# Fifty-two weight blocks of a two-block transformer layer, multiplied as whole float32 in place of three split products

## The chip, the cores and the metric

The kernel runs on one core of a Trainium2 chip. A core has a matrix engine (PE, TensorE; its weight loads are listed as PEld), a vector engine (DVE), an activation engine (ACT), a general engine (POOL, GpSimd) and a queue that starts transfers (SP). The metric is the device time of one execution in microseconds (us); less is better.

## The reference, cut to what matters

The reference is two transformer blocks, one after the other, over 256 tokens (and 16 learned "meta" tokens) of width 1024, all in float32. The change touches only the start of the first block:

```python
u = rms_norm(h, pre_mix_gain[l])
proj = u @ w_in[l]
qa, ka, va, qb, kb, vb, g = jnp.split(proj, SPLITS, axis=-1)
...
o_swa = windowed_gqa_sink_attention(qa, ka, va, attn_sink[l], pos, is_real)
...
o_diff = differential_attention(qb, kb, vb, lam, lambda_init, diff_subln_gain[l], is_key)
gates = jax.nn.sigmoid(g + b_gate[l])
merged = g_swa * (o_swa @ w_branch_swa[l]) + g_diff * (o_diff @ w_branch_diff[l])
h = h + rms_norm(merged @ w_out[l], post_mix_gain[l])
```

`w_in` is 1024 by 6656, so 52 blocks of 1024 by 128: 8 for `qa`, 4 for `ka` and `va`, 8 each for `qb`, `kb`, `vb`, and 16 for the gates. After that come the first block's feed-forward, and the whole second block (a delta-rule mixer, a sparse attention, a cross attention, a second feed-forward), which the change leaves alone.

## The kernel before

Activations lie transposed: a tile holds 128 features by the tokens. A weight block is 128 partitions by 1024 (eight pieces of 128 by 128, one for each 128 of the contraction). `raw_w` has SP load a block into `raw` (three buffers, 512 KB a block). `load_w` then splits it into two tiles of the rounded type float32r: `wh` is the block rounded (a copy on ACT) and `wl` is the rest, `raw - wh` (on DVE, or on POOL for every second block while `wshare[0]` is 2). Activations are split in the same way by `split` into `uh` and `ul`. `gemm` multiplies each of the eight pieces three times, `wh·uh + wh·ul + wl·uh`, so 24 matmuls a block into one PSUM bank. Twenty blocks (`kb`, `vb`, `ka`, `va`) take all 272 tokens, `us_k`; 32 (`qb`, `qa`, the gates) take 256, `us`.

What stands around these blocks is attention: eight differential heads (`diff_head`) and eight pairs of window heads (`swa_pair`), in the order of `ORDER`. Each takes scores on PE (the line of `scores`), maxima on DVE, exponentials on ACT, normalised weights on DVE (`am`, `pr`), transposes on PE into PSUM tiles `t`, a split of those on ACT and DVE, and the product with the values on PE. A query or key block, once multiplied, goes through `rope` (ACT, DVE, POOL) and a split. The blocks of head n+2 are multiplied after head n, and the gate blocks fill in between, as `GATES` says. At the end of the stage `branch_d` multiplies eight blocks `w_bd` and the merge multiplies eight blocks `w_bs`, with `gemm` in both versions. A 1 MB transfer of `memt` stands on SP's queue behind the last `w_bd` block; its squares and sums on POOL (`mem_split`) end in a small matmul, in `sums_tok`.

The program is laid out for each engine before it runs: a scheduler puts the instructions of each engine in one fixed order, and semaphores make them wait for one another. The start of the stage:

```python
AHEAD = 2
for n in range(AHEAD):
    prepare(n)
for n, (t, i) in enumerate(units):
    if t == "d":
        diff_head(i, qs.pop(0))
    else:
        swa_pair(i // 4, i % 4, qs.pop(0))
    if n + AHEAD < 16:
        prepare(n + AHEAD)
    for _ in range(GATES[n]):
        gate_of(fill.pop(0))
```

Of the kernel before, what the change touches and what calls it, by code (L numbers as in the profile page):

```python
# [16 lines left out]
F32 = mybir.dt.float32  # L17
# [3 lines left out]
AF = mybir.ActivationFunctionType  # L21
# [4 lines left out]
P = 128  # L26
NT = 256
NM = 16
NK = NT + NM
NP = NT + 32  # L30
D = 1024
KT = D // P
# [173 lines left out]

WSHARE = 2
ORDER = "ddssdsddsdssddss"  # L210
GATES = [int(c) for c in "0010202020302022"]
BDLAST = 0
# [8 lines left out]
def _program(tc, d, out):  # L221
    nc = tc.nc
    ctx = ExitStack()
    pe, act, dve, pool, sp = nc.tensor, nc.scalar, nc.vector, nc.gpsimd, nc.sync
# [7 lines left out]
    with ctx:  # L232
# [4 lines left out]
        gpool = new_pool(ctx, "gen")  # L237
        mm = new_pool(ctx, "mm", 2, PSUM)


        hT = rpool.tile([P, KT, NK], F32, name="hT", tag="resA")
# [14 lines left out]
        def G(n, j=0):  # L256
            o, w = _GC[n]
            return gcol[:, o + j:o + j + 1]
# [25 lines left out]
        def split(h, l, src, gain=None):  # L284

            if gain is None:
                m = act.activation(h, src, AF.Copy)
                dve.tensor_tensor(l, src, h.bitcast(F32), OP.subtract)
            else:
                m = act.activation(h, src, AF.Copy, scale=gain)  # L290
                dve.scalar_tensor_tensor(l, src, gain, h.bitcast(F32), OP.mult, OP.subtract)  # L291
            return m

        wcount, wshare, hshare, last_w = [0], [0], [0], [None]

        def raw_w(src, n):
            raw = wpool.tile([P, KT * P], F32, name="raw", tag="raw", bufs=3)
            last_w[0] = sp.dma_start(raw[:, :n * P], src)
            return raw
# [16 lines left out]
        def gemm(src, xs, n, use, first=True, last=True, ps=None, raw=None, late=()):  # L316

            kt = len(xs)
            h, l = load_w(src, kt, raw=raw)
            if ps is None:  # L320
                ps = mm.tile([P, 512], F32, name="mm", tag="mm")
            o = ps[:, :n]
            soon = [k for k in range(kt) if k not in late]
            steps = [(w, k, i) for ks in (soon, late) for w, i2 in ((h, 2), (l, 1)) for k in ks for i in range(i2)]
            for n_, (w, k, i) in enumerate(steps):
                pe.matmul(o, w[:, k * P:(k + 1) * P], xs[k][i], start=(first and n_ == 0),  # L326
                          stop=(last and n_ == len(steps) - 1))
            if last and use is not None:
                use(o)
            return ps  # L330

        def gemm_long(src, xs, n, use):

            ps = None
            for k in range(0, len(xs), KT):
                part = xs[k:k + KT]
                ps = gemm(src[:, k * P:(k + len(part)) * P], part, n, use, first=(k == 0),
                          last=(k + KT >= len(xs)), ps=ps)
# [59 lines left out]
        def new_u():  # L398
            uh = gpool.tile([P, KT, NK], F32R, name="uh", tag="uh")
            ul = gpool.tile([P, KT, NK], F32R, name="ul", tag="ul")  # L400
            return uh, ul
# [8 lines left out]
        apx = ExitStack()  # L410
        apool = new_pool(apx, "a")

        uh, ul = new_u()

        st = opool.tile([P, 512], F32, name="st", tag="o")
        for _ in range(WARM):
            tc.keep_in_program_order(pe.matmul(st[:, :P], one.to_broadcast([P, P]), one.to_broadcast([P, P]),
                                               start=True, stop=True))
        wfirst = [raw_w(d["w_kb"][0], KT)]
        for k in range(1, KT, 2):  # L420
            n = min(2, KT - k)
# [6 lines left out]
        ipool = new_pool(ist, "i", side="right")  # L428
        st = opool.tile([P, 512], F32, name="st", tag="o")
        for k in range(KT):  # L430
            split(uh[:, k, :], ul[:, k, :], hT[:, k, :], G("pre_mix", k))
            s0 = ipool.tile([P, NK], F32, name="s0", tag="s0", bufs=KT)
            pool.tensor_tensor(s0, hT[:, k, :], hT[:, k, :], OP.mult)
            pe.matmul(st[:, :NK], ones_d, s0, start=(k == 0), stop=(k == KT - 1))
# [2 lines left out]
        dve.tensor_copy(below_b, CA("below"))  # L437
        rs = gpool.tile([P, NK], F32, name="rs", tag="rs", bufs=2)
        rsqrt_chain(st[:, :NK], NK, rs)
        us = [(uh[:, k, :NT], ul[:, k, :NT]) for k in range(KT)]  # L440
        us_k = [(uh[:, k, :], ul[:, k, :]) for k in range(KT)]
        ist.close()

        gate = apool.tile([P, 16, NT], F32, name="gate")
# [45 lines left out]
        def bank():  # L490

            began[0] += 1
            return ppool.tile([P, 512], F32, name="s", tag="s") if began[0] <= 3 else None
# [5 lines left out]
        def key(o, kh, kl, eng):  # L499
            k = kpool.tile([P, NK], F32, name="kraw", tag="kraw", bufs=3)  # L500
            rope(o, k, ckt, skt, NK, eng)
            split(kh, kl, k)
# [8 lines left out]
        def key_tiles(name, bufs):  # L511
            return [kpool.tile([P, NK], F32R, name=name + e, tag=name + e, bufs=bufs) for e in ("_h", "_l")]

        kb, vb = {}, {}

        def keys_b(h):
            kb[h] = key_tiles("kb", 3)
            gemm(d["w_kb"][h], us_k, NK, lambda o: key(o, *kb[h], dve), ps=bank(),
                 raw=wfirst.pop(0) if wfirst else None)

        def padded(name, n, shape):
# [14 lines left out]
        def value(o, h, l, m, cols=slice(0, P)):  # L536

            v = next(vTs)
            dve.tensor_tensor(v[:, :NK], o, rs, OP.mult)
            t = tpool.tile([P, 512], F32, name="t", tag="t")  # L540
            pe.transpose(t[:, 0:128], v[:, 0:128], ident)
            pe.transpose(t[:, 128:256], v[:, 128:256], ident)
            tm = tpool.tile([P, 512], F32, name="t", tag="t")
            pe.transpose(tm[:32, :P], v[:, NT:], ident)
            t3 = t[:, 0:256].rearrange("p (a b) -> p a b", a=2)
            for hh, ll_, mm_, cc_ in zip(h, l, m, cols):
                act.activation(hh, t3[:, :, cc_], AF.Copy)
                dve.tensor_tensor(ll_, t3[:, :, cc_], hh.bitcast(F32), OP.subtract)
                stacked(mm_, tm[:32, cc_], 32)

        def values_b(h):
            vh = kpool.tile([P, 2, P], F32R, name="vb_h", tag="vb_h", bufs=3)
            vl = kpool.tile([P, 2, P], F32R, name="vb_l", tag="vb_l", bufs=3)
            vm = kpool.tile([96, P], F32R, name="vbm", tag="vbm", bufs=3)
            vb[h] = vh, vl, vm
            gemm(d["w_vb"][h], us_k, NK, lambda o: value(o, [vh], [vl], [vm], [slice(0, P)]), ps=bank(),
                 raw=wfirst.pop(0) if wfirst else None)

        def probs_t(pps):
# [74 lines left out]
        def query(src):  # L634
            q = [kpool.tile([P, NT], F32R, name="q" + e, tag="q" + e, bufs=3) for e in "hl"]

            def use(o):
                qr = kpool.tile([P, NT], F32, name="qraw", tag="qraw", bufs=2)
                rope(o, qr, cqt, sqt, NT)
                split(*q, qr)  # L640
            gemm(src, us, NT, use, ps=bank())
            return q

        os_h, os_l = [None] * 8, [None] * 8
# [36 lines left out]
        ka = [key_tiles("ka%d" % p, 1) for p in range(2)]  # L681
# [6 lines left out]

        def swa_keys():
            for p in range(2):  # L690
                gemm(d["w_kva"][p], us_k, NK, lambda o, p=p: key(o, *ka[p], pool))
            lo, hi = slice(0, 64), slice(64, P)
            for p in range(2):
                gemm(d["w_kva"][2 + p], us_k, NK, lambda o, p=p: value(
                    o, [va_h[:, :, p, i, c] for i, c in ((0, lo), (1, hi))],
                    [va_l[:, :, p, i, c] for i, c in ((0, lo), (1, hi))],
                    [vam[:, p, i, c] for i, c in ((0, lo), (1, hi))], [lo, hi]))

        def gate_of(j):
            gemm(d["w_gate1"][j], us, NT,  # L700
                 lambda o: dve.tensor_tensor(gate[:, j, :], o, rs[:, :NT], OP.mult))

        ods = [(od_h[:, k, :], od_l[:, k, :]) for k in range(8)]
# [3 lines left out]
            gemm(d["w_bd"][j], ods, NT, lambda o: act.activation(bd[:, j, :], o, AF.Copy))  # L707


        wshare[0] = WSHARE  # L710
        order = ORDER
        units = [(t, order[:i].count(t)) for i, t in enumerate(order)]
        qs, fill = [], list(range(16))
# [91 lines left out]
        for j in range(8):  # L805
            def use(o, j=j):
                t = mpool.tile([P, NT], F32, name="mt", tag="mt", bufs=2)
                dve.tensor_tensor(t, o, gate[:, j, :], OP.mult)
                dve.tensor_tensor(t, t, bd[:, j, :], OP.add)
                split(m_h[:, j, :], m_l[:, j, :], t)  # L810
# [18 lines left out]
        def post_norm(src_w, xs, gain, res, res_out, g_next):  # L829
# [12 lines left out]
            for j in range(8):  # L842
# [9 lines left out]
        us, rs = post_norm(d["w_out1"], [(m_h[:, k, :], m_l[:, k, :]) for k in range(8)],  # L852
                           "post_mix", hT, h1, "pre_ffn")

        def ffn_in(pool_, src_w, us, rs, f_h, f_l):
            for j in range(FT):
# [7 lines left out]
                def use_u(o, sg=sg, j=j):  # L864
# [44 lines left out]
        us, rs = post_norm(d["w_fo1"], [(f_h[:, k, :], f_l[:, k, :]) for k in range(FT)],  # L909
                           "post_ffn", h1, x1, "g_mix")  # L910
# [549 lines left out]
        for c in range(2):  # L1460
            gb = ppool.tile([P, 512], F32, name="s", tag="s")
            for h in range(4):
                pe.matmul(gb[:, h * P:(h + 1) * P], gg[:, 4 * c + h:4 * c + h + 1].to_broadcast([P, P]), triu,
                          start=True, stop=True)
# [62 lines left out]
        us, rs = residual(d["w_out2"], [(mix_h[:, k, :], mix_l[:, k, :]) for k in range(8)], x1, x2, "g_xattn", (0,1,2,3), 2)  # L1527
# [26 lines left out]
        for h in range(4):  # L1554
# [28 lines left out]
            o = opool.tile([P, 512], F32, name="o", tag="o")  # L1583
            o = o.rearrange("p (a b) -> p a b", a=2)
# [8 lines left out]
        us, rs = residual(d["w_xo"], [(ox_h[:, k, :], ox_l[:, k, :]) for k in range(8)], x2, x3, "g_ffn", (4,5,6,7), 2)  # L1593
# [49 lines left out]
        for qb in range(2):  # L1643
# [3 lines left out]
            for n, i in enumerate(own):  # L1647
                _, lo, w = parts[i]
                cols = slice(lo, lo + w)
                x = x3t[:, qb, cols]  # L1650
# [39 lines left out]
```

## Time and profile before

| what | value |
|---|---|
| median of three runs | 1033.79 us (1032.21 to 1034.55) |
| the profiled execution | 1033.08 us, of which the span from first to last instruction is 1031.3 us |
| PE busy in the span | 964.4 us (94%) |
| DVE busy | 771.9 us (75%) |
| ACT busy | 563.9 us (55%) |
| POOL busy | 369.0 us (36%) |
| granted TensorE clock, mean | 0.976 |

Matmuls are pipelined, so their busy time is not the time that each takes in a stream; the pace of a stream is read from the starts of consecutive matmuls in a timeline. A granted clock of 1.00 is the upper of the engine's two levels, 2.4 GHz, 0.50 the lower, 1.2 GHz; a mean between them is a stretch that had some of both. The stage that the change touches runs from the start to about 264 us.

### The profile page before, as it was taken

The numbers are of one execution on the slowest core, as the hardware profiler recorded it, in microseconds if no ns is written. First come the engines' busy times: TensorE is split into PE (matmuls) and PEld (weight loads), VectorE is DVE, ScalarE is ACT, GpSimd is POOL, SyncE is SP. The second block draws the span as 40 slices with busy tenths as digits, with TensorE's granted clock in tenths as the row PEclk, the third lists the DMA queues.
The fourth block names the chain that finished last, engine by engine and source line by source line (L and its number), as shares of the span: only waits on it lengthen the run. The fifth ranks groups of instructions, "written<-read, shape, count | busy, mean of one in ns | idle before, by whom it ended". The sixth has DMA issues, their size and how long they took to land.

```text
span 1031.3 us, 19437 instructions
## 1 busy us (share of the span) xinstructions
PE 964.4 (94%) x7532; PEld 916.8 (89%) x7532; DVE 771.9 (75%) x1477; ACT 563.9 (55%) x1111; POOL 369.0 (36%) x317
## 2 busy tenths in 40 slices
PE   9889999999969999999999778769999999999997
PEld 8779899998959989999999777668899999999986
DVE  7999888888696786666456899999688686656544
ACT  5566767667445655555554555435666565555433
POOL 6866458555590221212100755553021102121002
PEclk9999999999989999999999899799999999999999
DMA  6323333332444475555665331231035255555552
GB/s 236 124 102 108 119 106 117 106 124 103 164 143 161 146 242 177 189 186 181 212 209 179 123 123 62 83 122 63 2 104 183 103 181 188 184 185 186 184 191 94
DMA packets 42027, 149.32 MB, mean 145 GB/s; under 512 B 4728, under 2 KB 5376, under 8 KB 41808
## 3 DMA queue, kind: packets, MB, share of 16 engines
q1 hardware_dynamic: 40896, 145.47, 41.2%
q0 software_dynamic: 608, 2.03, 0.7%
q8 instruction: 59, 0.97, 0.4%
q10 hardware_dynamic: 432, 0.59, 0.2%
q14 instruction: 32, 0.26, 0.1%
HBM read 147.01 MB, written 1.06 MB: 144 GB/s over the span
## 4 chain that ended last, share of the span: by engine, by line
PE 67%; DVE 22%; ACT 3%; POOL 3%; issue 3%; DMA 2%; SPq 0%; DVEq 0%; ACTq 0%; POOLq 0%
PE mm L326 46%; DVE wl L313 3%; PE s L326 2%; PE ac L1624 2%; PE s L509 2%; PE ac L1628 2%; PE ac L1627 2%; ACT wh L311 1%; DVE acc L393 1%; DVE base L1129 1%; POOL memt L773 1%; DVE fg L843 1%; DVE ul L291 1%; DVE y L981 1%; PE o L589 1%
## 5 line engine op out<-in xcount | busy, mean ns | idle before, releaser
L311 ACT ACTIVATE wh<-raw 128x1024 fp32r<-128x1024 f32 (+1 forms) x266 | 279.3, 1053 | 230.0 <-PE mm L326 138.1
L326 PE MATMUL mm<-uh,wh 128*128 128x256 f32 (+1 forms) x1272 | 322.5, 289 | 11.9 <-DVE zp L975 7.6
L313 DVE TENSOR_TENSOR wl<-raw,wh 128x1024 fp32r<-128x1024 f32 (+1 forms) x219 | 272.6, 1247 | 77.5 <-ACT wh L311 76.3
L326 PE MATMUL mm<-ul,wh 128*128 128x256 f32 (+1 forms) x1272 | 320.1, 287 | 0.0
L326 PEld LDWEIGHTS mm<-uh,wh 128*128 128x128 f32 x1272 | 242.7, 191 | 16.7 <-issue 8.3
L326 PEld LDWEIGHTS mm<-ul,wh 128*128 128x128 f32 x1272 | 243.2, 191 | 1.1 <-issue 0.2
L326 PE MATMUL mm<-uh,wl 128*128 128x256 f32 (+1 forms) x1272 | 184.5, 284 | 0.0
L326 PEld LDWEIGHTS mm<-uh,wl 128*128 128x128 f32 x1272 | 165.3, 190 | 0.9 <-issue 0.2
L313 POOL TENSOR_TENSOR wl<-raw,wh 128x1024 fp32r<-128x1024 f32 x53 | 127.7, 2415 | 90.4 <-ACT wh L311 79.6
L862 POOL TENSOR_TENSOR sg<-sg,rs 128x256 f32<-128x256 f32 x44 | 49.6, 1130 | 233.6 <-ACT sg L861 228.6
L866 DVE TENSOR_TENSOR ft<-mm,sg 128x256 f32<-128x256 f32 x42 | 17.8, 424 | 52.0 <-PE mm L326 51.4
L326 PE MATMUL mm<-f_h,wh 128*128 128x256 f32 x176 | 41.1, 276 | 0.0
L326 PE MATMUL mm<-f_l,wh 128*128 128x256 f32 x176 | 41.1, 276 | 0.0
L860 DVE TENSOR_TENSOR sg<-mm,rs 128x256 f32<-128x256 f32 x40 | 16.9, 424 | 31.8 <-PE mm L326 31.8
L1624 PE MATMUL ac<-wh,f_h 128*128 128x512 f32 (+1 forms) x110 | 38.4, 349 | 0.0
L1627 PE MATMUL ac<-wh,f_l 128*128 128x512 f32 (+1 forms) x110 | 38.1, 347 | 0.0
L1628 PE MATMUL ac<-wl,f_h 128*128 128x512 f32 (+1 forms) x110 | 37.8, 347 | 0.0
L326 PEld LDWEIGHTS mm<-f_h,wh 128*128 128x128 f32 x176 | 33.0, 188 | 0.0
L326 PEld LDWEIGHTS mm<-f_l,wh 128*128 128x128 f32 x176 | 33.0, 188 | 0.0
L844 POOL TENSOR_TENSOR x<-fg,h 128x256 f32<-128x256 f32 x8 | 8.8, 1127 | 66.6 <-DVE fg L843 66.6
L1540 POOL TENSOR_TENSOR kx_l<-kx,kx_h 128x512 fp32r<-128x512 f32 x4 | 6.8, 1720 | 66.8 <-ACT kx_h L1539 66.8
L393 DVE TENSOR_TENSOR acc<-acc,sq 128x256 f32<-128x256 f32 x42 | 27.1, 646 | 0.4
(546 smaller groups left out, 2234.9 us busy)
## 6 DMA issues: line engine op xcount, KB each, us to landing
raw<-w_gu SPq DMA_DIRECT2D x88, 512.0 KB, 3.3
raw<-w_dn SPq DMA_DIRECT2D x22, 512.0 KB, 3.2
raw<-w_pr SPq DMA_DIRECT2D x20, 512.0 KB, 3.3
raw<-w_gate SPq DMA_DIRECT2D x16, 512.0 KB, 3.2
raw<-w_out SPq DMA_DIRECT2D x16, 512.0 KB, 3.2
raw<-w_fo SPq DMA_DIRECT2D x16, 512.0 KB, 3.7
raw<-w_kb SPq DMA_DIRECT2D x8, 512.0 KB, 3.3
raw<-w_vb SPq DMA_DIRECT2D x8, 512.0 KB, 3.3
```

The lines of the kernel that those rows point to most:

```text
L291: dve.scalar_tensor_tensor(l, src, gain, h.bitcast(F32), OP.mult, OP.subtract)
L311: act.activation(h[:, :kt * c], raw[:, :kt * c], AF.Copy)
L313: eng.tensor_tensor(l[:, :kt * c], raw[:, :kt * c], h[:, :kt * c].bitcast(F32), OP.subtract)
L326: pe.matmul(o, w[:, k * P:(k + 1) * P], xs[k][i], start=(first and n_ == 0), stop=(last and n_ == len(steps) - 1))
L393: dve.tensor_tensor(acc, acc, s[:, :n], OP.add)
L509: pe.matmul(os[c], a[half[c], tok], b[half[c]], start=(n == 0), stop=(last and n == 2))
L860: dve.tensor_tensor(sg, o, rs, OP.mult)
L862: pool.tensor_tensor(sg, sg, rs, OP.mult)
L866: dve.tensor_tensor(t, o, sg, OP.mult)
L1624: m = pe.matmul(o, f_h[:, k, tok], h[:, cols], start=(k == 0), stop=False)
L1627: pe.matmul(o, f_l[:, k, tok], h[:, cols], start=False, stop=False)
L1628: pe.matmul(o, f_h[:, k, tok], l[:, cols], start=False, stop=(k == FT - 1))
```

## The change

A new function `gemm_whole` multiplies each of the eight pieces once, the raw float32 block with the whole float32 activation: eight matmuls a block in place of 24, and neither `wh` nor `wl` is made. All 52 blocks of the first block's projections go through it. The activation `u` is written by one ACT operation for each 128 features, and not split. `wshare[0]` is no longer set in this stage, so the splits of the `w_bd` blocks, which stay as they were, are all on DVE.

```diff
-WSHARE = 2
...
+        def gemm_whole(src, xs, n, use, ps=None, raw=None):
+
+            if raw is None:
+                raw = raw_w(src, len(xs))
+            if ps is None:
+                ps = mm.tile([P, 512], F32, name="mm", tag="mm")
+            o = ps[:, :n]
+            for k, x in enumerate(xs):
+                pe.matmul(o, raw[:, k * P:(k + 1) * P], x, start=(k == 0), stop=(k == len(xs) - 1))
+            use(o)
...
-        uh, ul = new_u()
+        u = gpool.tile([P, KT, NK], F32, name="u", tag="uh")
...
-            split(uh[:, k, :], ul[:, k, :], hT[:, k, :], G("pre_mix", k))
+            act.activation(u[:, k, :], hT[:, k, :], AF.Copy, scale=G("pre_mix", k))
...
-        us = [(uh[:, k, :NT], ul[:, k, :NT]) for k in range(KT)]
-        us_k = [(uh[:, k, :], ul[:, k, :]) for k in range(KT)]
+        us = [u[:, k, :NT] for k in range(KT)]
+        us_k = [u[:, k, :] for k in range(KT)]
...
-            gemm(d["w_kb"][h], us_k, NK, lambda o: key(o, *kb[h], dve), ps=bank(),
+            gemm_whole(d["w_kb"][h], us_k, NK, lambda o: key(o, *kb[h], dve), ps=bank(),
...
-            gemm(src, us, NT, use, ps=bank())
+            gemm_whole(src, us, NT, use, ps=bank())
...
-            gemm(d["w_gate1"][j], us, NT,
+            gemm_whole(d["w_gate1"][j], us, NT,
...
-        wshare[0] = WSHARE
```

The other calls (`w_vb`, `w_kva`) change in the same way.

The scheduler lays the stage out anew. On POOL, where the first keys and queries are rotated, this stood before (`wl` is the split of a block, `ropem`, `rot`, `kraw` and `qraw` the steps of `rope`):

```order
L313 TENSOR_TENSOR wl<-raw,wh 128x1024 x3
L484 TENSOR_TENSOR ropem<-rawq,ckt 128x272
L484 TENSOR_TENSOR ropem<-rawq,cqt 128x256
L485 TENSOR_TENSOR rot<-rot,sqt 128x256
L486 TENSOR_TENSOR kraw<-ropem,rot 128x272
L486 TENSOR_TENSOR qraw<-ropem,rot 128x256
L313 TENSOR_TENSOR wl<-raw,wh 128x1024
L484 TENSOR_TENSOR ropem<-rawq,ckt 128x272
```

and this stands there now:

```order
L494 TENSOR_TENSOR ropem<-rawq,ckt 128x272
L496 TENSOR_TENSOR kraw<-ropem,rot 128x272
L494 TENSOR_TENSOR ropem<-rawq,cqt 128x256
L495 TENSOR_TENSOR rot<-rot,sqt 128x256
L496 TENSOR_TENSOR qraw<-ropem,rot 128x256
L494 TENSOR_TENSOR ropem<-rawq,ckt 128x272
```

The rotations no longer stand behind splits of weights.

On SP, the fourth block on and the constants before, with the engines that each transfer waits for (names of DMA queues begin with DMAHW):

```order
L298 DMA raw<-w_kb 128x1024 [waits DMAHW3_49,DVE_49]
L424 DMA ca_75<-const_a 128x544 [waits DMAHW4_49]
L298 DMA raw<-w_vb 128x1024 [waits DMAHW6_49,DMAHW5_49,Pool_49]
L298 DMA raw<-w_qb 128x1024 [waits DMAHW0_49,DVE_49]
L298 DMA raw<-w_qa 128x1024 [waits DMAHW7_49,DMAHW3_49,Pool_49]
```

and now:

```order
L434 DMA ca_75<-const_a 128x544 [waits DMAHW3_49]
L297 DMA raw<-w_kb 128x1024 [waits DMAHW4_49,PE_49]
L297 DMA raw<-w_vb 128x1024 [waits DMAHW6_49,DMAHW5_49,PE_49]
L297 DMA raw<-w_qb 128x1024 [waits DMAHW0_49,PE_49]
L297 DMA raw<-w_qa 128x1024 [waits DMAHW7_49,DMAHW4_49,PE_49]
```

A raw buffer was given back by the split (DVE or POOL), and is given back now by the last matmul that reads it (PE). From the fourth block on each transfer waits for the block three before it.

On PE, around the first scores (`s<-kb_h,qh` and the like are scores of the first head; `t<-base,vT` is a transpose of values), before:

```order
L541 MATMUL t<-base,vT_208 128x128
L542 MATMUL t<-base,vT_208 128x128
L544 MATMUL t<-base,vT_208 32x128
L326 MATMUL mm<-uh,wh 128x256
...
L326 MATMUL mm<-uh,wh 128x256
L509 MATMUL s<-kb_h,qh 128x272 x3
L326 MATMUL mm<-ul,wh 128x256
...
L326 MATMUL mm<-ul,wh 128x256
L509 MATMUL s<-kb_h,ql 128x272 x2
L509 MATMUL s<-kb_l,qh 128x272 x2
```

and now:

```order
L339 MATMUL mm<-u,raw 128x272 x8
L519 MATMUL s<-kb_h,qh 128x272 x3
L519 MATMUL s<-kb_h,ql 128x272
L339 MATMUL mm<-u,raw 128x256 x8
L519 MATMUL s<-kb_h,ql 128x272
L519 MATMUL s<-kb_l,qh 128x272 x2
L551 MATMUL t<-base,vT_199 128x128
L552 MATMUL t<-base,vT_199 128x128
L554 MATMUL t<-base,vT_199 32x128
```

The first scores stand beside whole blocks of eight matmuls, with a full block between the two halves of the scores. From the feed-forward of the first block on, the order on PE is the same in both.

## Rows read from the trace of the kernel before

**Rows 1.** Stretches: us, busy of PE, PEld, DVE, ACT, POOL (instructions), PEclk, DMA share, GB/s.

```profile
20.00:264.50 244.50, 234.48 (x1796) 215.44 (x1795) 215.77 (x446) 155.53 (x392) 152.39 (x136) 0.99 0.33 114
36.00:44.00 8.00, 8.00 (x52) 7.55 (x49) 6.62 (x14) 4.78 (x12) 4.77 (x5) 0.79 0.20 72
140.00:150.00 10.00, 9.07 (x57) 8.21 (x56) 8.18 (x19) 5.43 (x17) 3.74 (x3) 0.83 0.30 107
```

**Rows 2.** Waits of PE, 5 to 265 us: in total, times, longest; eleven lines, 10.6 us.

```profile
PE t L576 <- DVE vam L532: 2.9, 1, 2.9
PE s L509 <- DVE ql L288: 2.0, 1, 2.0
PE t L567 <- DVE am L610: 1.8, 1, 1.8
...
PE o L589 <- DVE r L607: 0.2, 1, 0.2
```

**Rows 3.** PE's timeline in streams of split products: start us, us, engine, line.

```profile
23.66 0.29 PE L326 MATMUL mm<-uh,wh 128*128 128x272 f32 x1
...
25.56 0.29 PE L326 MATMUL mm<-ul,wh 128*128 128x272 f32 x1
...
27.19 0.28 PE L326 MATMUL mm<-uh,wh 128*128 128x256 f32 x1
...
28.97 0.28 PE L326 MATMUL mm<-ul,wh 128*128 128x256 f32 x1
```

**Rows 4.** PE's timeline around two whole-float32 matmuls, each recorded as x2.

```profile
14.40 0.62 PE L434 MATMUL st<-s,base 128*128 128x272 f32 x2
14.66 0.61 PE L326 MATMUL s<-uh,wh 128*128 128x272 f32 x2
15.11 0.28 PE L326 MATMUL s<-ul,wh 128*128 128x272 f32 x1
...
346.34 0.59 PE L343 MATMUL st<-acc,base 128*128 128x256 f32 x2
346.58 0.47 PE L326 MATMUL mm<-mem_l,wh 128*128 128x256 f32 x1
346.89 0.28 PE L326 MATMUL mm<-mem_h,wh 128*128 128x256 f32 x1
```

**Rows 5.** Groups, 0 to 265 us: busy us, mean ns, then idle before and its releasers.

```profile
L313 POOL TENSOR_TENSOR wl<-raw,wh 128x1024 fp32r<-128x1024 f32 x27 | 65.0, 2406 | 41.8 <-ACT wh L311 41.8
L311 ACT ACTIVATE wh<-raw 128x1024 fp32r<-128x1024 f32 x56 | 59.2, 1059 | 18.7 <-PE mm L326 10.7 <-DMA raw<-w_kb 2.5 <-DMA raw<-w_qb 1.6
L313 DVE TENSOR_TENSOR wl<-raw,wh 128x1024 fp32r<-128x1024 f32 x28 | 38.2, 1365 | 2.5 <-ACT wh L311 2.5
L291 DVE SCALAR_TENSOR_TENSOR ul<-hT,base,uh 128x272 fp32r<-128x272 f32 x8 | 8.2, 1092 | 0.0
```

**Rows 6.** Transfers of weights, 0 to 265 us: KB each, median us to landing.

```profile
raw<-w_gate SPq DMA_DIRECT2D x16, 512.0 KB, 3.2
raw<-w_kb SPq DMA_DIRECT2D x8, 512.0 KB, 3.3
```

**Rows 7.** The end of the stage: timeline rows of DVE, SP, POOL, and PE.

```profile
266.33 2.32 DVE L313 TENSOR_TENSOR wl<-raw,wh 128x1024 fp32r<-128x1024 f32 x1 [1.62 <-ACT wh L311]
...
269.06 0.42 SPq L767 DMA_DIRECT2D memt<-memT  x1
...
280.00 5.77 POOL L773 TENSOR_TENSOR memt<-memt 128x256 f32<-128x256 f32 x4 [2.20 <-DVE mem_l L771]
...
308.20 0.59 PE L380 MATMUL st<-base,memt 128*128 128x1 f32 x2 [7.88 <-POOL memt L775]
```

**Rows 8.** PE's timeline where it comes back from scores to a block.

```profile
32.38 0.52 PE L509 MATMUL s<-kb_h,qh 64*128 64x272 f32 x3
32.83 0.38 PE L326 MATMUL mm<-ul,wh 128*128 128x256 f32 x1
33.05 0.28 PE L326 MATMUL mm<-uh,wh 128*128 128x256 f32 x1
```

More of the change, by code (lines that the diff above doesn't have):

```diff
@@ L555, in values_b @@
             vb[h] = vh, vl, vm
-            gemm(d["w_vb"][h], us_k, NK, lambda o: value(o, [vh], [vl], [vm], [slice(0, P)]), ps=bank(),
+            gemm_whole(d["w_vb"][h], us_k, NK, lambda o: value(o, [vh], [vl], [vm], [slice(0, P)]), ps=bank(),
                  raw=wfirst.pop(0) if wfirst else None)
@@ L690, in swa_keys @@
             for p in range(2):
-                gemm(d["w_kva"][p], us_k, NK, lambda o, p=p: key(o, *ka[p], pool))
+                gemm_whole(d["w_kva"][p], us_k, NK, lambda o, p=p: key(o, *ka[p], pool))
             lo, hi = slice(0, 64), slice(64, P)
             for p in range(2):
-                gemm(d["w_kva"][2 + p], us_k, NK, lambda o, p=p: value(
+                gemm_whole(d["w_kva"][2 + p], us_k, NK, lambda o, p=p: value(
                     o, [va_h[:, :, p, i, c] for i, c in ((0, lo), (1, hi))],
```

## The prediction, made before the run

> **What bounds the kernel now.** I read the stretches first, then PE's waits, then PE's timeline. The stage of the change ends at about 264 us. From 20 to 264.5 us PE is busy for 234.5 of 244.5 us and DVE for 215.8, while ACT and POOL have room (155.5 and 152.4) [rows 1]. The reader should see that two engines are near their limit, and ask which of them waits. PE waits for anything only 10.6 us in all of 5 to 265 us, in eleven lines, and almost all of that is for DVE: a transposed value, a query, a normalised head [rows 2]. So PE sets the pace of this stage, and DVE holds it up now and then. Two short stretches have a lower granted clock, 0.79 over 8 us and 0.83 over 10 us [rows 1]; a mean like that is a part of the stretch at 1.2 GHz in place of 2.4, and each follows an idle piece of PE (the 2.0 us wait for `ql` ends at 35.7 us).
>
> The pace itself stands in the timeline, not in the busy times, since matmuls overlap. Sixteen split products of 272 columns start between 23.66 and 25.56 us, so 1.90/15 = 0.127 us each; sixteen of 256 columns between 27.19 and 28.97 us, so 0.119 us [rows 3]. A block of 24 takes 3.04 us (272 columns) or 2.85 us (256).
>
> At the end of the stage PE waits 7.9 us for POOL's sums over `memt`, up to 308.2 us. That chain starts with the transfer of `memt`, at 269.06 us, which SP issues behind the last `w_bd` block; and that block waits for the split of an earlier one, which ends at 268.65 us [rows 7]. So what counts is when PE is through the projections and the first two `w_bd` blocks; work on PE after that has 7.9 us of slack and neither version changes it.
>
> **The change, part by part.**
>
> *Matmuls: the cost.* The trace has no stream of whole float32 products of these sizes, but single ones between split products. Such a matmul is recorded as two instructions. At 346.34 us one of 256 columns starts, then one split product, and the next starts at 346.89: 0.55 us, less 0.119 for the split product, leaves 0.431 us [rows 3, 4]. For 272 columns: 14.40 to 15.11 us is 0.71, less two at 0.127, leaves 0.457 us [rows 3, 4]. Eight make 3.45 us for a block of 256 columns (+0.60) and 3.66 us for one of 272 (+0.62). With 32 and 20 blocks that is 19.2 + 12.4 = **+31.6 us** on PE, all of it on the path, since PE sets the pace. So one whole product costs 3.6 split products and not four. The Trainium skill ("FP8 and Floating Point Precision", TensorE Precision Notes) says that true FP32 takes four passes through the array and the reduced one truncates to a single read; by the plain count the price would be 4/3 of the split one, and I keep that as a rival with its own chance, though the rows above stand against it.
>
> *Splits: what falls away.* On ACT 52 copies of 1.06 us (55 us); on DVE 26 splits of 1.37 us and the eight of `u`, 8.2 us (44 us); on POOL 26 of 2.41 us (63 us) [rows 5]. None of these engines sets the pace, so none of it counts by itself. It counts where PE waits for DVE. DVE falls from 215.8 us to some 175 us in a stage that gets longer, and POOL's rotations no longer stand behind splits (the order shows it). I take 7.5 of PE's 10.6 us of waits as given back; the bounds are 0 (the waits are latencies of chains that the new order cuts just as fine) and 10.6. **-7.5 us.**
>
> *Clock.* The two low stretches cost 8 x 0.21 and 10 x 0.17, together 3.4 us [rows 1]. Each stands behind idle time on PE; if that goes, they go. Bounds 0 and 3.4; I take **-3 us**, since it hangs on the term before it.
>
> *Fewer re-entries.* When PE comes back from scores to a block, the first matmul takes 0.22 us to the next start in place of 0.119 [rows 8]. A split block could be entered afresh twice, at its first `wh` and at its first `wl` matmul, since each has something to wait for; a whole block only once. 52 places at 0.10 us are 5.2 us at most. Many of the `wl` groups run on without a gap, so the least is nothing: **-2 us.**
>
> *The raw buffers.* They are now released by PE and no longer by the split. A transfer takes 3.2 to 3.3 us from issue to landing [rows 6]. After the release PE still has two loaded blocks, 6.9 us or more. That covers it: **0**, with the loss as a rival. Behind a late transfer on SP stand only further blocks, and `memt` at the end.
>
> *The last splits.* All eight `w_bd` splits are on DVE now, four of them more than before, and POOL has none. The split that releases the last block took 2.32 us beside a split on POOL, against a mean of 1.37 [rows 5, 7]. The `memt` transfer, and all behind it, comes sooner by **-1 us** (0 to -1). The extra four splits on DVE, some 5 us, lie beside PE's seven remaining blocks; without this cover they would cost PE at most these 5 us, of which 7.9 us of slack hide all.
>
> *The start.* The first two blocks run on PE as features arrive, between statistics; `ul` splits on DVE fall away there, and PE's work grows by 0.6 us a block. I take these to be even: 0, in the bounds of the terms above.
>
> **Sum.** 31.6 - 7.5 - 3 - 2 - 1 = +18.1 us. On the profiled execution's 1033.1 us that is 1051.2 us; it lies 0.7 us below the median of the three runs, so against the median it is +1.7%. What follows the stage is laid out the same on PE and only moves. With every gain at its bound (10.6, 3.4, 5.2, 1) it is +11.4, 1045 us; with none, +31.6, 1065 us.
>
> **Rivals.**
>
> *Nothing is given back on PE's waits.* The order is fixed ahead, and heads are chains over four engines; new waits take the place of the old ones. For it: the waits in the trace are few and each has its own cause, so they are not simply DVE's load [rows 2]. Against it: nine tenths of them are for DVE, which gets lighter by a fifth. The waits and the low clock stay: 1033.1 + 31.6 - 3 = 1062 us.
>
> *Four full passes.* A whole product at four times the pace of a split one: 0.475 and 0.507 us, +0.95 and +1.01 us a block, +50.6 us in all; with the same gains, 1033.1 + 50.6 - 13.5 = 1070 us. Against it: the 0.431 and 0.457 us measured, which agree with each other. For it: those are single matmuls, and a long stream may load weights worse. The Trainium skill's count of passes, named above, is this case.
>
> *Weights come late.* The first three blocks end close together on PE, since the scheduler interleaves the first two with the arriving features; then only one block of 3.45 us lies between a release and the need, and 3.3 us plus the issue is about as long. A few microseconds at the start, or one now and then later: 1055 to 1060 us. It decides if a transfer lands later than two blocks after its release.
>
> *The other side: faster.* The whole products stream faster than the single ones. The average whole matmul costs 0.441 us by the rows, (32 x 0.431 + 20 x 0.457)/52. The sum of +18.1 us spread over 416 of them is 0.044 us each, so the change pays below 0.397 us. At the price of the three split products in its place (0.366 us) only the gains would be left: 1033.1 - 13.5 = 1020 us. For it: a neighbour of another kind stands on each side in the rows, and may cost something at the change. Against it: two sizes give the same price a column.
>
> **Chances.** The forecast (1043 to 1061 us) 0.62; no waits given back 0.14; late weights 0.08; four passes 0.08; faster 0.05; the rest, about even, 0.03. Three of the four rivals make it slower too. The range of 1041 to 1066 us leaves out four passes and the faster case, and some of the edges. From no change this kernel can be told apart by about 0.2%, 2 us. So: slower 0.92, the same 0.03, faster 0.05.
>
> **What would show it.** Right: PE in the stage has two records for each whole matmul, starts 0.215 us apart at 256 columns; the stage's end (`memt` issued) moves from 269 to about 287 us; PE's waits up to there fall to about 3 us and the granted clock is 1.00; DVE's busy time in the stage falls by 35 to 45 us, POOL's by about 65. Wrong: a pace of 0.24 us a record (four passes); PE waiting for transfers `raw`; a sum of waits for DVE of 10 us or more; or a stage that ends before 269 us.

## Result and the profile after

The changed kernel takes 1050.62 us (median of four runs, 1047.54 to 1051.69) against 1034.04 us for the kernel before: 1.0157 times as long, 95% interval 1.0145 to 1.0169, 16.6 us more by the medians. Its profiled execution took 1051.69 us with a span of 1049.9 us.

The stretches of the changed kernel: the stage to the same time as in [rows 1], the stage to its last whole product, the eight `w_bd` blocks behind it, and 166 us of the second block (columns as in [rows 1]).

```profile
20.00:264.50 244.50, 244.50 (x1307) 200.58 (x1306) 133.26 (x395) 106.26 (x322) 74.20 (x105) 1.00 0.32 104
20.00:267.80 247.80, 247.80 (x1323) 203.47 (x1322) 135.94 (x403) 108.92 (x329) 74.20 (x105) 1.00 0.33 107
267.80:298.60 30.80, 29.09 (x243) 27.69 (x241) 23.15 (x40) 15.58 (x31) 9.70 (x11) 1.00 0.51 174
609.00:775.00 166.00, 138.49 (x1015) 124.46 (x1014) 143.51 (x402) 81.64 (x212) 64.96 (x44) 0.91 0.21 70
```

PE is now busy all through the stage, and the granted clock is 1.00, where [rows 1] has 0.79 and 0.83 in two places. DVE and POOL have fallen to 133 and 74 us in 244.5. The waits of PE from 5 to 265 us, eleven lines and 10.6 us in [rows 2], are one line:

```profile
PE s L339 <- ACT u L441: 0.5, 1, 0.5
```

The pace of the whole products, from PE's timeline (start us, us; each product is recorded as two, so x16 is one block):

```profile
20.76 3.83 PE L339 MATMUL mm<-u,raw 128*128 128x272 f32 x16
24.43 0.27 PE L551 MATMUL t<-base,vT 128*128 128x128 f32 x1
...
262.80 4.48 PE L339 MATMUL mm<-u,raw 128*128 128x256 f32 x20
267.11 0.59 PE L632 MATMUL st<-sq,base 128*128 128x256 f32 x2
```

Sixteen records of 272 columns take from 20.76 to 24.43, 3.67 us a block. Twenty of 256 columns take from 262.80 to 267.11, so 0.2155 us each (4.31/20) and 3.45 us a block. These are the prices that the prediction took from two single matmuls [rows 3, 4].

The end of the stage, the lines that answer to [rows 7], and ahead of them where SP starts the `w_bd` transfers:

```profile
256.00 0.33 SPq L297 DMA_DIRECT2D raw<-w_bd  x1
...
281.60 0.38 SPq L776 DMA_DIRECT2D memt<-memT  x1
...
292.27 2.57 POOL L782 TENSOR_TENSOR memt<-memt 128x256 f32<-128x256 f32 x1 [17.04 <-ACT bd L717]
...
320.43 0.80 PE L390 MATMUL st<-base,memt 128*128 128x1 f32 x3 [9.47 <-POOL memt L784]
```

`memt` is issued 12.5 us later than before and PE's sums over it start 12.2 us later, as much as the stage is longer (267.8 against 255.6 us). The span grew by 18.6 us; the rest arose behind this place. The stretches in the kernel before, and where SP starts the `w_bd` transfers there:

```profile
20.00:255.60 235.60, 225.67 (x1722) 206.94 (x1721) 208.44 (x432) 150.05 (x379) 148.11 (x131) 0.99 0.33 115
255.60:283.10 27.50, 27.41 (x239) 27.10 (x238) 18.75 (x35) 13.09 (x27) 14.57 (x9) 1.00 0.46 163
594.00:760.00 166.00, 139.40 (x1045) 125.16 (x1044) 146.91 (x408) 84.50 (x219) 65.00 (x44) 0.94 0.21 73
```

```profile
231.77 37.24 SPq L298 DMA_DIRECT2D raw<-w_bd  x8
```

The stretch of the `w_bd` blocks takes 30.8 us in place of 27.5, and SP starts their first transfer at 256.00 and not at 231.77 us, since it may do so only when PE has read earlier whole blocks. But this lengthens nothing: PE still comes to the sums over `memt` too early and waits there, 9.5 us where it waited 7.9. What does add is the place of these sums. Behind `w_bd` stand eight `w_bs` blocks, with 16 products that read `os_h` in each. Here they are counted ahead of the sums and behind them, in the kernel before and then in the changed kernel (this view has no POOL):

```profile
283.20:305.00 21.80, 14.76 (x80) 12.28 (x80) 0.00 (x0) 0.00 (x0) 0.96 0.38 121
305.00:319.50 14.50, 10.75 (x48) 9.26 (x48) 0.00 (x0) 0.00 (x0) 0.71 0.42 149
```

```profile
298.00:318.00 20.00, 11.88 (x64) 9.96 (x64) 0.00 (x0) 0.00 (x0) 0.93 0.39 132
318.00:334.50 16.50, 13.10 (x64) 11.31 (x64) 0.00 (x0) 0.00 (x0) 0.78 0.41 128
```

So the scheduler put the sums behind the fifth block before, and behind the fourth now: four blocks follow the wait in place of three. PE's first merged product, the next work behind them, before and now:

```profile
319.59 0.37 PE L326 MATMUL mm<-m_h,wh 128*128 128x256 f32 x1
```

```profile
334.62 0.28 PE L325 MATMUL mm<-m_h,wh 128*128 128x256 f32 x1
```

That is 15.0 us later, so the place of the sums cost 2.8 us beyond the 12.2. From there to the end of the span it is 711.7 us before and 715.3 now, 3.6 us more; in the second block, which the change does not touch, the granted clock is 0.91 in place of 0.94. These 3.6 us are not shown to belong to the change: in the profiled run of experiment 3, with 36 whole blocks, the same part takes 711.6 us, and in that of the kernel before with its sums moved (experiment 4) 717.0. Of the four runs of the changed kernel the quickest (1047.54 us) has a mean granted clock of 0.980, the profiled one 0.975.

### The profile page after: what moved, and what is told of

It reads as the page before. It is cut to its first block, busy times and chain, and to the rows that moved or that the text cites. A ratio compares the mean times of both kernels' runs of the same rounds, so it can differ in the third digit from the quotient of the medians.

```text
span 1049.9 us, 18417 instructions
## 1 busy us (share of the span) xinstructions
PE 990.9 (94%) x7116; PEld 916.2 (87%) x7116; DVE 693.3 (66%) x1447; ACT 519.9 (50%) x1059; POOL 280.4 (27%) x287
## 4 chain that ended last, share of the span: by engine, by line
PE 79%; DVE 12%; POOL 3%; DMA 2%; ACT 2%; issue 1%; SPq 0%; DVEq 0%; ACTq 0%; POOLq 0%
PE mm L325 38%; PE mm L339 17%; PE s L519 3%; PE s L325 2%; PE ac L1633 2%; PE ac L1637 2%; PE ac L1636 2%; PE o L599 1%; DVE acc L403 1%; DVE wl L312 1%; PE s L339 1%; DVE base L1138 1%; DVE fg L852 1%; POOL memt L784 1%; DVE y L990 1%
## 5 line engine op out<-in xcount | busy, mean ns | idle before, releaser
L310 ACT ACTIVATE wh<-raw 128x1024 fp32r<-128x1024 f32 (+1 forms) x214 | 224.4, 1051 | 219.1 <-PE mm L325 132.2
L325 PE MATMUL mm<-uh,wh 128*128 128x256 f32 x880 | 218.4, 286 | 11.9 <-DVE zp L984 9.2
L325 PE MATMUL mm<-ul,wh 128*128 128x256 f32 x880 | 217.7, 285 | 0.0
L339 PE MATMUL mm<-u,raw 128*128 128x256 f32 (+1 forms) x784 | 187.7, 387 | 0.0
L325 PEld LDWEIGHTS mm<-uh,wh 128*128 128x128 f32 x880 | 168.1, 191 | 14.0 <-issue 9.6
L325 PEld LDWEIGHTS mm<-ul,wh 128*128 128x128 f32 x880 | 168.5, 191 | 0.3 <-issue 0.2
L339 PEld LDWEIGHTS mm<-u,raw 128*128 128x128 f32 x784 | 143.6, 190 | 22.5 <-issue 0.8
L325 PE MATMUL mm<-uh,wl 128*128 128x256 f32 x880 | 122.9, 281 | 0.0
L325 PEld LDWEIGHTS mm<-uh,wl 128*128 128x128 f32 x880 | 112.3, 189 | 0.1
L312 POOL TENSOR_TENSOR wl<-raw,wh 128x1024 fp32r<-128x1024 f32 x23 | 55.5, 2426 | 42.0 <-ACT wh L310 23.6
L869 DVE TENSOR_TENSOR sg<-mm,rs 128x256 f32<-128x256 f32 x40 | 17.0, 424 | 31.7 <-PE mm L325 31.6
```

The costliest lines, as they stand in the source:

```text
L310: act.activation(h[:, :kt * c], raw[:, :kt * c], AF.Copy)
L312: eng.tensor_tensor(l[:, :kt * c], raw[:, :kt * c], h[:, :kt * c].bitcast(F32), OP.subtract)
L339: pe.matmul(o, raw[:, k * P:(k + 1) * P], x, start=(k == 0), stop=(k == len(xs) - 1))
L869: dve.tensor_tensor(sg, o, rs, OP.mult)
```

## Experiments

Times are given as the ratio to the kernel before, run on the same chip between the runs of the experiment; 0.1% is 1 us. **Theory**: on PE the whole products cost some 30 us, and the splits that fall away give back some 11 us of waits and low clock. The rivals are named with each run.

**1. Splits kept, read by nobody.** In `gemm_whole`, and `wshare[0] = 2` as before:

```diff
+            load_w(src, len(xs), raw=raw)
```

> The changed kernel, but each of the 52 whole blocks is also split as before (copy on ACT, subtraction on DVE and POOL in turn), and nobody reads the two halves. The matmuls stay eight whole ones a block. Theory (PE's waits went because DVE and POOL got lighter): with the splits back the waits of about 10 us and the half clock behind them come back, 1058 to 1064 us, and PE again waits for DVE in the stage. Rival (the waits went because a whole block keeps PE busy 0.6 us longer, and the chains of the heads have more time): the splits cost nothing, 1049 to 1053 us.

Measured: 1050.66 us, 1.0167 (1.0153 to 1.0181). By the time alone the rival has it: the splits cost at most a microsecond or so. PE's waits from 5 to 265 us, and then the stretch from 20 to 264.5 us:

```profile
PE t L579 <- DVE am L622: 1.3, 1, 1.3
PE mm L341 <- DVE vT L551: 0.7, 1, 0.7
```

```profile
20.00:264.50 244.50, 242.51 (x1282) 197.27 (x1281) 189.61 (x411) 148.29 (x366) 144.54 (x129) 1.00 0.32 105
```

DVE and POOL carry nearly what they carried before, and PE waits 2.0 us and not 10.6. But the scheduler also laid out the end of the stage otherwise: PE's sums over `memt` now stand behind the last `w_bs` matmul, and the 9.5 us wait is gone.

```profile
329.51 1.16 PE L326 MATMUL mm<-os_h,wl 128*128 128x256 f32 x8
330.51 0.50 PE L392 MATMUL st<-base,memt 128*128 128x1 f32 x4
```

So two things may cancel here; experiment 5 takes them apart.

**2. The pace of before without the subtractions.** 24 split products a block, all from the rounded copy `wh` of the weight and the rounded `u`; neither `wl` nor `ul` exists, so the small parts of the 52 products are left out.

```diff
+            act.activation(h, raw, AF.Copy)
...
+                pe.matmul(o, h[:, k * P:(k + 1) * P], xs[k], start=(n_ == 0), stop=(n_ == 3 * len(xs) - 1))
```

> The other corner: 24 split products a block as before, but all of them from the rounded copies of the weight and the activation; the subtractions on DVE and POOL are left out, so the small parts of the 52 products are not computed. Theory (on PE the matmuls alone cost 31.6 us, and the waits stay away because DVE and POOL are light): 1050.6 - 31.6 = 1019 us, 1016 to 1024. Rival (a faster PE runs into the same waits whatever DVE does): the time of the kernel before, 1030 to 1035 us.

Measured: 1021.86 us, 0.9882 (0.9866 to 0.9898). PE waits for nothing from 5 to 265 us, and its stretch up to the last block is full:

```profile
20.00:240.00 220.00, 220.00 (x1700) 202.31 (x1699) 138.96 (x399) 150.42 (x377) 75.64 (x104) 1.00 0.34 117
```

At the pace of split products the subtractions cost 1.18%, 12 us, and some 3 us more if one allows for the sums over `memt`, which stand behind the fourth `w_bs` block here too. From here to the changed kernel, which has them at the same place, it is 1.0157 - 0.9882 = 2.75%, 28 us, for the matmuls. The copies on ACT are still made here, and they give the raw buffers back sooner; but PE's waits up to the first merged product are the same within 1 us in both kernels, so the 28 us are work of PE.

**3. Only the gates split.** `gemm` again for `w_gate1`, with a split copy of `u` beside the whole one; 36 blocks stay whole.

> Only the 16 gate blocks go back to split products, with their splits on ACT, DVE and POOL; the other 36 blocks stay whole. Theory (each block of 256 columns costs PE 0.60 us): 16 x 0.60 = 9.6 us less, and up to 16/52 of the 13 us of waits and clock come back, 4 us: 1041 to 1046 us. Rival (the loss sits at the end of the stage and not in the blocks): 1049 to 1052 us.

Measured: 1038.62 us, 1.0059 (1.0045 to 1.0072), 12 us less than the changed kernel and 2 to 7 below what was expected. PE waits for nothing in the stage here either, so none of the waits came back. Behind the last block PE has no idle time:

```profile
258.00:290.00 32.00, 32.00 (x275) 31.45 (x274) 21.76 (x41) 16.69 (x33) 18.72 (x13) 1.00 0.44 149
```

On the path stands `memt`. It is issued at 274.06 us, 7.5 sooner than in the changed kernel, and PE's sums start at 313.42, 7.0 sooner, so not all of the 9.6 us for the blocks arrives there. But the sums stand behind the fifth `w_bs` block again, as in the kernel before, and one block less follows them: the first merged product starts at 324.81 us, 9.8 sooner. The rest of the 12 us lies in what follows, which no change touched.

**4. Sums over `memt` late.** In the changed kernel, and later in the kernel before:

```diff
-        sums_tok(st, memt[:, 0, :], ones_d, 2)
+        with tc.issue_after(last_mm[0].ins):
+            sums_tok(st, memt[:, 0, :], ones_d, 2)
```

> The changed kernel, but PE's sums over memt are issued behind the last w_bs matmul and not between the w_bs blocks; four blocks of 2.8 us then cover the 9.5 us for which PE waited there. Theory (what PE loses at that place is a wait in the wrong place of its order): 9 to 10 us less, 1040 to 1043 us. Rival (the w_bs blocks or what reads them wait for POOL as well, so the wait only moves): 1048 to 1052 us.

> The kernel before, with the sums over memt behind the last w_bs matmul on PE, as in the run before this one for the changed kernel. Theory (both kernels lose a wait of 8 to 9.5 us at this place, and a half clock behind it): 7 to 9 us less than the kernel before, 1024 to 1027 us, faster than both kernels; the price of the change measured without this place is then some 16 to 17 us. Rival (PE of the kernel before has other waits to fall into there): 1030 to 1034 us.

Measured: changed kernel 1041.8 us, 1.0080 (1.0066 to 1.0094), as the theory has it. Kernel before 1030.72 us, 0.9966 (0.9954 to 0.9978), half of what was expected. Its PE waits from 280 to 345 us:

```profile
PE mm L327 <- DVE wl L314: 3.0, 2, 1.7
PE mm L327 <- DVE m_l L288: 2.2, 2, 1.6
PE mm L327 <- DVE wh L310: 1.1, 2, 0.5
```

The 7.9 us wait is gone, but of these 6.3 us only 2.2 were there before, so half of the gain is lost within 30 us. There was a wait in the wrong place of the order in both kernels, but it is worth 0.8% in one and 0.3% in the other; so 0.4% of the difference between the two kernels is this wait and the block more behind it. With the sums at the same place in both kernels the change costs 1.0080 - 0.9966 = 1.14%, 12 us, which is what the stage grew by.

**5. Both corners again, without that wait.** Experiments 1 and 2 with the sums late, the `w_bd` splits on DVE in both.

> The changed kernel with the 52 unread splits as in the first experiment, but the splits of the w_bd blocks on DVE alone, as in the changed kernel, and the sums over memt forced behind w_bs; it differs from the run at 1041.8 us only by the unread splits. Theory (the splits cost PE time also at the pace of whole products, and the first experiment hid it, since its order happened to have the sums behind w_bs and so saved the wait): 1048 to 1052 us. Rival (at the pace of whole products the splits are hidden): 1040 to 1044 us.

> 24 split products a block from the rounded copies alone, no subtractions (the small parts of the 52 products are left out), and the sums over memt behind w_bs. Theory (the 9.5 us wait for POOL stands here too): 1021.9 - 9 = 1013 us, 1011 to 1015; the matmuls alone then cost 1041.8 - 1013 = 29 us. Rival (nothing left to cover the wait at this pace): 1019 to 1023 us.

Measured: 1047.48 us, 1.0130 (1.0116 to 1.0143), just under the theory's range and above the rival's; and 1015.11 us, 0.9812 (0.9798 to 0.9825), the theory's upper end. With these the four corners stand in one order of the sums, in per cent against the kernel before:

| | split products | whole products | the matmuls cost |
|---|---|---|---|
| with the splits' work | -0.34 | +1.30 | 1.64 (17 us) |
| without subtractions | -1.88 | +0.80 | 2.68 (28 us) |
| the splits cost | 1.54 (16 us) | 0.50 (5 us) | |

With the sums where the scheduler put them (behind the fifth `w_bs` block in the kernel before, the eighth in experiment 1, the fourth in the other two) the same table reads 0, +1.67, -1.18 and +1.57. That gives 17 and 28 us again for the matmuls, but 12 and 1 us for the splits, which compares kernels of unlike order; the table above does not. So theory and rival of the first experiment each hold a part. Splits cost 16 us when PE runs at the pace of split products, and 5 us when it runs whole ones.

**6. More raw buffers.** `bufs=5` or 4 for `raw`, sums late.

> The run at 1041.8 us (changed kernel, sums late) with five raw buffers in place of three. Theory (no block of the 52 waits for its transfer; only the w_bd blocks at the end of the stage do, up to 4.5 us on the chain of waits, part of which PE feels): 0 to 3 us less, 1039 to 1042 us. Rival (transfers of weights are late throughout): 5 us less or more, below 1037 us.

> The changed kernel, four raw buffers, sums late; with three it took 8.7 us more than the kernel before on the same chip, with five 1.7 us more. Theory (each further buffer brings the memt transfer forward by about one w_bd block): between the two, 3 to 6 us above the kernel before. Rival (the first further buffer frees SP altogether): 1 to 2 us above it.

> The kernel before with four raw buffers in place of three and the sums over memt behind w_bs (five buffers don't fit beside its other tiles). Theory (a further buffer lets SP issue the w_bd blocks and memt behind them earlier, so POOL's chain over memt ends earlier and the merged products wait less): 4 to 7 us less than with the sums alone moved, 6 to 11 us below the kernel before. Rival (only in the changed kernel, where PE holds the raw buffers, does a further one help): 3 to 5 us below the kernel before, as with the sums alone.

Measured: changed kernel with five 1036.31 us, 1.0028 (1.0011 to 1.0045); with four 1043.28 us, 1.0087 (1.0066 to 1.0109), no gain over three; kernel before with four 1028.42 us, 0.9955 (0.9939 to 0.9971), against 0.9966 with three. Five came out at the rival's time, though not by the rival's cause: where PE waited in the stage is unchanged, since it hardly waited. SP's timeline with three buffers (the changed kernel with the sums late):

```profile
256.12 25.16 SPq L298 DMA_DIRECT2D raw<-w_bd  x8
281.37 0.38 SPq L777 DMA_DIRECT2D memt<-memT  x1
```

with four:

```profile
250.36 29.71 SPq L298 DMA_DIRECT2D raw<-w_bd  x8
280.16 0.38 SPq L777 DMA_DIRECT2D memt<-memT  x1
```

and with five:

```profile
245.18 24.50 SPq L298 DMA_DIRECT2D raw<-w_bd  x8
269.78 0.37 SPq L777 DMA_DIRECT2D memt<-memT  x1
```

With five, `memt` leaves 11.6 us sooner, and with it POOL's chain on which the merged products depend: PE's waits from 280 to 345 us fall to one of 0.7 us. With four it leaves only 1.2 us sooner. So neither expectation for four held. Why the fifth buffer does what the fourth does not can be read from DVE's splits of the first `w_bd` blocks. The last of the eight transfers takes the buffer of the fifth block when there are three buffers, of the fourth block when there are four, of the third when there are five. With four buffers, the third and the fourth split, and then the last transfer:

```profile
263.61 1.21 DVE L313 TENSOR_TENSOR wl<-raw,wh 128x1024 fp32r<-128x1024 f32 x1
278.49 1.23 DVE L313 TENSOR_TENSOR wl<-raw,wh 128x1024 fp32r<-128x1024 f32 x1 [0.17 <-ACT wh L311]
```

```profile
279.74 0.33 SPq L298 DMA_DIRECT2D raw<-w_bd  x1
```

With five, the third split and the last transfer, which then waits for PE's reads and no longer for a split:

```profile
258.94 1.23 DVE L313 TENSOR_TENSOR wl<-raw,wh 128x1024 fp32r<-128x1024 f32 x1 [0.36 <-ACT wh L311]
```

```profile
269.35 0.33 SPq L298 DMA_DIRECT2D raw<-w_bd  x1
```

The fourth split follows the third by 14.9 us, since `wh` and `wl` have three buffers each, and a fourth can be written only when PE is through with a `w_bd` block (the copy to `wh` that the fourth split needs starts at 277.40 us); the fifth split follows the fourth at once. So the fourth buffer saves one split, and only the fifth gets around the gap. This is read from the traces; no run changed the number of `wh` and `wl` buffers. In the kernel before, the fourth buffer's gain of 0.1% is within the intervals, as the rival has it (4.7 us below the kernel before).

**7. Which blocks are whole.** Four buffers and the gates split; five buffers and only the 20 blocks of keys and values whole. Sums late in both.

> 36 blocks whole and the 16 gates split, four raw buffers, sums late. Theory (cost by the block: 28 us measured over 52 blocks without splits, and few splits are hidden while PE runs whole products): 16 x 0.54 = 8.6 us less than the next kernel but one (52 whole, four buffers). Rival (what is whole and what is split does not matter by the block, only where the order puts things): within 3 us of it.

> Only the 20 blocks of 272 columns whole (keys and values), queries and gates split, five raw buffers, sums late. Their matmuls cost about 20 x 0.56 = 11 us more than split. Theory (what the splits cost PE is spread evenly, 15.6 us over 52 blocks, so 6 us come back): 4 to 7 us above the kernel with no whole block, four buffers and sums late. Rival (DVE holds PE up only above some load, and the first blocks taken off it give back most, 10 us or more): within 2 us of that kernel, or faster.

Measured: 1035.75 us, 1.0022 (1.0007 to 1.0037), 0.65% or 7 us below 52 whole blocks with four buffers, so about the 8.6 us of the cost by the block. And 1027.31 us, 0.9930 (0.9915 to 0.9945), beside 0.9955 (0.9939 to 0.9971) with no whole block and four buffers. It is faster than the kernel before and the changed kernel; from the kernel with no whole block it can't be told apart, since the intervals overlap. Its stretch up to the last block:

```profile
20.00:254.40 234.40, 233.11 (x1589) 203.01 (x1589) 179.06 (x422) 137.81 (x367) 126.15 (x124) 1.00 0.36 116
```

DVE still has 179 us of work, and PE waits 1.3 us. The 20 blocks cost PE some 11 us by the rate above, and that is given back. It came out at the rival's time, but its cause, that the first blocks taken off DVE are worth the most, is not shown: the fifth buffer is in this run and not in the one it stands beside, and in the changed kernel going from three buffers to five was worth 0.5%, 5 us.

## Why the prediction was right, and where its steps were off

The forecast was 1051.2 us, the median is 1050.62. The mechanism holds: PE sets the pace of the stage, a whole block costs more than a split one, and the work that goes from DVE and POOL gives back a part of that, by the experiments more than half. That the number is so close is luck: two errors of some 6 us cancel. Step by step:

- **Matmuls and re-entries.** Predicted +31.6 - 2 = 29.6 us, measured 28 us twice (corners without subtractions). The pace is right to 0.01 us a block. The difference fits the re-entries: the bounds were 0 and 5.2, and 3.6 would make up the sum. No run takes them by themselves.
- **Waits and clock.** Predicted -7.5 - 3 - 1 = -11.5 us, measured -12 us in experiment 2, whose sums stand one block sooner, and -16 with the sums at the same place. PE's waits fell by 10.1 of 10.6 us and the clock to 1.00, so both terms are close to their upper bounds. But the reason given, that DVE gets lighter, is only one of two. At the pace of whole products the waits fall to 2.0 us even with all splits kept. Each of the two is enough nearly by itself, so they don't add, and the rival "no waits given back" was wrong for a reason that the prediction didn't have.
- **Raw buffers: 0.** Right within the stage, where PE waits for no transfer. Behind it the first `w_bd` transfer moves from 232 to 256 us and the `w_bd` blocks take longer, but `memt`, which counts, is issued only 0.3 us later than the longer stage alone would have it. So the change of who releases the buffers cost next to nothing, though five buffers in place of three would have brought a gain (experiment 6).
- **The last splits.** Predicted -1 us for `memt`; it moved by as much as the stage, so nothing of this is seen.
- **"What follows the stage is laid out the same on PE and only moves."** This step failed. The stage itself got 12.2 us longer, near the lower bound of 11.4. Behind it the sums over `memt` stand one `w_bs` block sooner, which cost 2.8 us, and what follows the merged products took 3.6 us longer in the profiled run, with a lower granted clock; PE's order is the same there from the feed-forward on, and the time of this part differs between runs of other kernels too. The forecast of +18.1 for +18.6 in the profiled execution (+16.6 in the medians) came out of a stage that was 6 us better and a rest that was 6 us worse.
- **Signs.** Two records 0.2155 us apart: yes. Waits of about 3 us: 0.5. Clock 1.00: yes. POOL about -65: -74 up to the last block. `memt` issued at 287: 281.6, sooner, since the gains were larger. DVE -35 to -45: it fell by 72 us up to the last block (208.4 to 135.9), half as much again as the splits' 46 [rows 5]; see the last section.
- **Four full passes, the rival.** Out: 0.431 us for 256 columns is 3.6 split products. The count of the Trainium skill ("FP8 and Floating Point Precision", TensorE Precision Notes) is not refuted by that. At 2.4 GHz, the granted level throughout the stage, 0.431 us is 1034 cycles, 4.04 for each column, and the split product's 0.119 us is 1.12. That would fit four passes of one cycle a column; the rival's mistake was to price each of them like a split product. No run here shows the passes themselves.
- **The other rivals.** No weights came late in the stage, and none of the kernels with whole blocks throughout was faster than the kernel before.

## What to carry to other kernels

Price an operation from its starts in a stream, even if the trace has only one or two of them between others: here two singles gave the price of 416. When a slower operation on the pacing engine replaces work elsewhere, the waits it saves and the waits its slowness hides are the same waits; count them once, and look for a part of the blocks for which the exchange is even (here keys and values, with a fifth buffer), not for all or none. Follow a buffer that changes its releaser past the end of the stage, to the transfers that stand behind it in the queue. And compare the order of both kernels behind the stage too: here the scheduler moved one wait ahead by a block, and this cost 2.8 us.

## What the runs showed of the hardware

Some DVE operations take as long as the POOL split beside them. The kernel before, timeline of DVE, then of POOL:

```profile
99.67 2.24 DVE L288 TENSOR_TENSOR ql<-qraw,qh 128x256 fp32r<-128x256 f32 x1
...
118.48 2.37 DVE L665 TENSOR_TENSOR es<-nb,nsink 128x2 f32<-128x2 f32 x1
```

```profile
99.18 2.45 POOL L313 TENSOR_TENSOR wl<-raw,wh 128x1024 fp32r<-128x1024 f32 x1
...
118.44 2.39 POOL L313 TENSOR_TENSOR wl<-raw,wh 128x1024 fp32r<-128x1024 f32 x1 [4.41 <-ACT wh L311]
```

The first, 0.42 us long elsewhere in the same stage (at 114.51 us), and the second, a subtraction of two columns, start beside POOL's split and end within 0.3 us after it. The group of `ql` in the whole stage, before and in the changed kernel, where POOL has no such splits:

```profile
L288 DVE TENSOR_TENSOR ql<-qraw,qh 128x256 fp32r<-128x256 f32 x16 | 14.3, 893 | 1.8 <-ACT qh L287 1.8
```

```profile
L287 DVE TENSOR_TENSOR ql<-qraw,qh 128x256 fp32r<-128x256 f32 x16 | 7.4, 460 | 5.2 <-ACT qh L286 5.1
```

The Trainium skill ("Trainium Architecture — The Big Picture", What this means for kernel authors) says that the port pair of DVE and GpSimd is the one place on the engines' side of SBUF that is contended, and that it is an exclusive lock; these rows agree. It would explain why DVE's busy time fell by half as much again as its own splits take, and it is a likely reason why the splits held up the heads' chains: the 2.0 us wait for `ql` is among PE's waits [rows 2]. No run moved POOL's splits alone, so how much of the 16 us is the lock and how much is DVE's own work was not measured.
